# A new order for the opening of a hybrid encoder layer: contraction rows outside, rounding on ScalarE, sums on VectorE

## The chip, the cores and the metric

The kernel runs on one core of a Trainium2 chip. A time is the device time of one launch in microseconds (us); the measure is the median over several launches. One further launch is recorded by the hardware profiler, and all views of the profile are of that launch. "us from the start" counts from the first instruction of that record.

## The reference

One layer of a bidirectional encoder on x of 2048 rows and 1024 columns, in float32. Cut to what the change touches:

```python
mod = silu(c) @ w_mod + b_mod                       # 6 vectors of 1024: shift1, scale1, gate1, ...
hmix = rms_norm(x, g_norm1) * (1 + scale1) + shift1
proj = hmix @ w_in                                  # 2832 columns
q_a, k_a, v_a, q_m, k_m, v_m, o_m, gates = split(proj)
# windowed attention on q_a, k_a, v_a; two-way mLSTM on q_m, k_m, v_m with the 16 gate columns
x = x + gate1 * (concat(att, h_m) @ w_out)
x = x + gate2 * (silu(g) * u) @ w_ffn_out           # SwiGLU on a second modulated norm
return rms_norm(x) * g_final
```

So nothing of `proj` can be formed before `scale1` and `shift1` are there, and these need 8 MB of `w_mod` (two of its six blocks of 1024 columns, 4 MB each).

## The kernel before, in words

Every product is made to nearly float32 accuracy out of three products of a rounded type (`fp32r`): an operand t is split in a high part, t rounded, and a low part, t minus the high part, and `mm3` (L55 to L58) adds high x high, high x low and low x high. So each operand costs a rounding and a subtraction before TensorE can use it.

The first stage makes the columns of `proj` that are wanted with rows on the partitions: 272 (attention values, gates, one head of mLSTM values; tile `pa`) and 384 (the other mLSTM values; tile `pv`). `nat_mm` (L396) does this for one tile of 128 rows: for each of eight blocks k of the contraction three products into `pa`, then the same for `pv`. The weights of block k are the tiles `wnh` and `wnl` (high and low, split in `split_nat`, L339, from the raw `wnr`); the rows are the transposed, modulated x, the tiles `hT`.

A block of 512 rows of x (`xt`) is scaled by its inverse root mean square, and then for each k: four transposes on TensorE (L182), one ScalarE instruction that applies scale and shift and writes `ntmp` (L183), a VectorE copy that rounds (L189) and a VectorE subtraction (L190). All that is `turned_split` (L185).

The modulation is made in halves z of 512 columns, since block k = 4z..4z+3 needs half z only. `mod_sum` (L205) is a generator of three steps. The first multiplies the rows of `w_mod` by silu(c) and adds them up on VectorE (L212, L214: eight instructions for a whole sum). The second adds over the partitions on TensorE, directly to a column (L229), or, if the first four blocks are left to TensorE (`n_pe` is 4), by L219 and L220 to a row which ScalarE copies (L222) and L225 turns into a column. The third adds the bias (L236). With m = 1 for the scale and m = 0 for the shift, `n_pe` is 4 for (1, 0) and for (0, 1). `scales(z)` (L327) then makes the factor that L183 uses.

The order of the opening is written out (L403 to L437): both sums of half 0, the weights of half 0, blocks k = 0 to 3 of x, then all products of these four blocks for row tiles 0, 1 and 2, which have six banks of PSUM between them (`ops`); then half 1 of the sums, of the weights and of x. After L438 come the products of blocks 4 to 7 for tiles 0 to 2, then tiles 3 to 15. TensorE's order is the program's order throughout the kernel. The other engines keep the program's order up to L438 too; after it a planner places their instructions, and it can place them into gaps ahead of L438.

From L980 on the convolution tiles of the mLSTM are projected (L497, `proj_mm`), 24 products into a bank `g` of which there are two. ScalarE and VectorE empty it (L524, and L511, L512 in `sides`, seven products after its last). Beside this runs `gates` (L836): a chain of small VectorE and ScalarE steps with four little TensorE steps. It yields the number of the product at which its next step is put into every queue. `rps` (L885) adds chunk totals, a scan follows on eight partitions, `cps` (L899, L900) spreads the result, and at last the values are transposed (L924) and stored with four DMAs (L920, L921) for the mLSTM, whose first load of them (L602) comes after product 252. `w_out_ops` (L945) runs on GpSimd at the same time.

Of the kernel before, what the change touches and what calls it, by code (L numbers as in the profile page):

```python
# [11 lines left out]
F32 = mybir.dt.float32  # L12
# [9 lines left out]
P = 128  # L22
T = 2048
D = 1024
KT = D // P
# [11 lines left out]
def hybrid_layer_kernel(  # L37
# [14 lines left out]
    def bank(tag, name):  # L52
        return pp.tile([P, 512], F32, tag=tag, name=name, bufs={"g": 2, "a": 2, "b": 1, "c": 2, "d": 1}[tag])
# [108 lines left out]
    def squares(pl, xt):  # L162

        ssq = pl.tile([P, 4], F32, tag="ssq", name="ssq")
        for i in range(4):
            jk = pl.tile([P, D], BF16, tag="junk", name="junk", bufs=1)
            act.activation(jk, xt[i], AF.Square, accum_out=ssq[:, i:i + 1])
        return ssq

    def scaled(xt, r, on_act=False):  # L170

        for i in range(4):
            if on_act:
                act.activation(xt[i], xt[i], AF.Copy, scale=r[:, i:i + 1])
            else:
                dve.tensor_scalar(xt[i], xt[i], r[:, i:i + 1], None, MUL)
# [8 lines left out]
    def turned_split(pl, xt, k, gs, shift, dst):  # L185

        t = pl.tile([P, 512], F32, tag="ntmp", name="ntmp", bufs=2)
        turned(t, xt, k, "bd"[k % 2], gs, shift)
        dve.tensor_copy(dst(0, k), t)  # L189
        dve.tensor_tensor(dst(1, k), t, dst(0, k).bitcast(F32), SUB)  # L190
# [14 lines left out]
    def mod_sum(pl, m, z, ws_, n_pe):  # L205


        acc = pl.tile([P, 512], F32, tag="macc", name="macc")
        for k in range(n_pe, KT):
            w = ws_[k // 2][:, k % 2, :]  # L210
            if k == n_pe:
                dve.tensor_scalar(acc, w, sc_col[:, k:k + 1], None, MUL)  # L212
            else:
                dve.scalar_tensor_tensor(acc, w, sc_col[:, k:k + 1], acc, MUL, ADD)  # L214
        yield True
        if n_pe:
            ps = bank("b", "modrow")
            for k in range(n_pe):
                pe.matmul(ps[:1, :], sc_col[:, k:k + 1], ws_[k // 2][:, k % 2, :], start=k == 0, stop=False)  # L219
            pe.matmul(ps[:1, :], ones[:, 0:1], acc, start=False, stop=True)  # L220
            row = pl.tile([1, 512], F32, tag="mrow", name="mrow", bufs=1)
            act.activation(row, ps[:1, :], AF.Copy)  # L222
            ps = bank("b", "modps")
            for k in range(4):
                pe.matmul(ps[:, k:k + 1], row[:, k * P:(k + 1) * P], ones[:1, 0:1], start=True, stop=True)  # L225
        else:
            ps = bank("d", "modps")
            for k in range(4):
                pe.matmul(ps[:, k:k + 1], acc[:, k * P:(k + 1) * P], ones[:, 0:1], start=True, stop=True)  # L229
        yield True  # L230
        mod_bias(m, z, ps)
        yield True
# [44 lines left out]
    with tc.tile_pool(name="sw", bufs=2, side="right", reuse_waits="tile") as sw:  # L277
# [58 lines left out]
                sp.dma_start(r[1 + i], w4[:, 2 * i:2 * i + 2, C_VM:C_VM + 512])  # L336
            return r

        def split_nat(z, r):  # L339
            ks = BD[z]  # L340
            act.activation(wh[:, ks, :144], r[0], AF.Copy)
            dve.tensor_tensor(wl[:, ks, :144], r[0], wh[:, ks, :144].bitcast(F32), SUB)
            for i in range(4):
                k, v = 4 * z + i, r[1 + i // 2][:, i % 2]
                act.activation(wh[:, k, 144:], v, AF.Copy)
                (pool, dve)[i % 2].tensor_tensor(wl[:, k, 144:], v, wh[:, k, 144:].bitcast(F32), SUB)

        def norm1(n, xt):
            hT.append(Kt(n, f"hT{n}"))
# [58 lines left out]
        for src, o, n in ((g_norm2, O_G2, 8), (conv_b, O_CB, 8), (conv_w[0], O_CW, 24), (g_attn_out, O_GA, 4), (g_mlstm_out, O_GM, 4)):  # L408
            sp.dma_start(rows[1][o - N_A:o - N_A + n, :], src.rearrange("o (a b) -> (o a) b", b=P))
        hT.append(Kt(0, "hT0"))  # L410
        ms = {(m, z): mod_sum(s1, m, z, wm[m, z], 4 if m == 1 - z else 0) for z in range(2) for m in (1, 0)}
        ssq = squares(s1, xts[0])
        r = rsqrt(s1, ssq, 4, D, "rs")
        next(ms[1, 0])
        scaled(xts[0], r, True)
        next(ms[0, 0])
        next(ms[1, 0])
        next(ms[1, 0])
        next(ms[0, 0])
        next(ms[0, 0])  # L420
        scales(0)
        split_nat(0, wn[0])
        ops = {i: (bank("gga"[i], "pa"), bank("acc"[i], "pv")) for i in range(3)}
        for k in range(4):
            turned_split(s1, xts[0], k, gs1, mod[:, 0, :], hT[0])
        for i in range(3):
            deque(nat_mm(0, i, *ops[i], range(4)), 0)
        next(ms[1, 1])
        split_nat(1, wn[1])
        next(ms[1, 1])  # L430
        next(ms[1, 1])
        next(ms[0, 1])
        next(ms[0, 1])
        next(ms[0, 1])
        scales(1)
        for k in range(4, KT):
            turned_split(s1, xts[0], k, gs1, mod[:, 0, :], hT[0])  # L437
# [5 lines left out]
        for n in range(NB):  # L443
            if n + 1 < NB:
                nrm = norm1(n + 1, xts[n + 1])
                next(nrm)
            if n == 0:
                xts.append(load_x(3))
            if n == 1:
                vecs = mod_row(2)  # L450
                columns_of(1, N_A, N_B)
                dve.tensor_scalar(cvw, cols[:, O_CW:O_CW + 24].rearrange("p (j k) -> p j k", j=3), 0.5, None, MUL)
                dve.tensor_scalar(cvb, cols[:, O_CB:O_CB + KT], 0.5, None, MUL)
                dve.tensor_scalar(gml, cols[:, O_GM:O_GM + HM], 0.5, None, MUL)
            if n + 1 == NB:
                w_first = proj_cols(C_KM)
            for i in range(4):
                tt = 4 * n + i
                if tt < 3:
                    pa, pv = ops[i]  # L460
                else:
                    pa, pv = bank("g", "pa"), bank("a", "pv")
                ev = EVERY[n][i]
                for j, _ in enumerate(nat_mm(n, i, pa, pv, range(4 if tt < 3 else 0, KT))):
# [371 lines left out]
    def gates():  # L836
# [43 lines left out]
        for sl, j in ((lo_, 127), (hi_, 0)):  # L880
            dve.tensor_scalar(st[sl, 0], spot[sl], b[sl, j:j + 1], None, MUL)
            dve.scalar_tensor_tensor(st[sl, 1], spot[sl], cm[sl, j:j + 1], st[sl, 0], MUL, ADD)
        yield 62
        ps = bank("c", "rps")
        pe.matmul(ps[:8, :2 * NT], pick, st.rearrange("p j c -> p (j c)"), start=True, stop=True)  # L885
        sr = s2.tile([8, 2, NT], F32, name="sr", bufs=1)
# [3 lines left out]
        dve.tensor_copy(rw[:, 0, 1:], mn[:, :-1])  # L890
        dve.tensor_tensor(rw[:, 1], sr[:, 0], mn, SUB)
        dve.tensor_tensor(rw[:, 2], rw[:, 1], rw[:, 0], ADD)
# [4 lines left out]
        dve.tensor_tensor(rx, rowm, rw[:, 2].unsqueeze(1).to_broadcast([8, 8, NT]), MUL)  # L897
        ps = bank("c", "cps")
        pe.matmul(ps[:, :2 * NT], rowm.rearrange("q r c -> q (r c)"), rw[:, :2].rearrange("q j c -> q (j c)"), start=True, stop=True)  # L899
        pe.matmul(ps[:, P:2 * P], ones[:8, :], rx.rearrange("q r c -> q (r c)"), start=True, stop=True)  # L900
# [1108 lines left out]
```

## Time and profile before

| | |
|---|---|
| median of three runs (lowest, highest) | 2263.84 us (2262.03, 2265.5) |
| the profiled execution: time, span | 2262.92 us, 2261.1 us |
| TensorE busy | 2219.7 us, 98% |
| VectorE, ScalarE, GpSimd busy | 1611.6, 1061.4, 1041.5 us |

The difference between the profiled time and the span, 1.8 us, lies around the instructions. In a row of the timeline stand the start, the duration, the engine, the line, the operation, what it writes and reads, its shape, how many instructions the row takes together, and in brackets how long the engine had been idle and what ended that. In a row of the windows each engine has its busy time and number of instructions, then comes the granted clock of TensorE (1.00 is full), the share of the DMA engines and the rate. Matmuls overlap, so that the pace of a stream is the distance of the starts and not the duration.

### The profile page before, as it was taken

What the parts mean: (1) busy time and instruction counts of PE and PEld (TensorE: products, weight loads), DVE (VectorE), ACT (ScalarE), POOL (GpSimd) and SP (SyncE); (2) the same over time, 40 slices, a digit from 0 to 9 for tenths busy, and PEclk for the clock granted to TensorE, in tenths of its full rate; (3) what the DMA queues carried; (4) which work ended last, traced back from release to release, by engine and by line L of the source; (5) the groups of instructions that cost most, each with busy time, mean ns of one, the idle gap of its engine ahead of it and who ended that gap; (6) DMA issues with size and microseconds to landing.
All of it is one profiled execution on the core that took longest, in us unless ns stands there. A gap on an engine that the chain in (4) does not pass through costs nothing.

```text
span 2261.1 us, 32357 instructions
## 1 busy us (share of the span) xinstructions
PE 2219.7 (98%) x10818; PEld 1858.9 (82%) x10818; DVE 1611.6 (71%) x2942; ACT 1061.4 (47%) x2209; POOL 1041.5 (46%) x904
## 2 busy tenths in 40 slices
PE   7999999999999999999999999999999999999998
PEld 4997888888788878888888888888888888888887
DVE  6776667656688887886667777777766665785694
ACT  5433665554678746354445444433333333233452
POOL 1016535334344333436666565467665663692020
PEclk8999999999999999999999999999999999999999
DMA  8566755685766576764343455534333374543462
GB/s 323 169 208 200 227 166 170 190 241 168 209 185 189 175 242 209 266 234 156 107 144 110 153 182 170 170 126 140 98 112 98 112 260 141 172 149 95 145 217 93
DMA packets 337063, 391.28 MB, mean 173 GB/s; under 512 B 20874, under 2 KB 234234, under 8 KB 336896
## 3 DMA queue, kind: packets, MB, share of 16 engines
q1 hardware_dynamic: 335616, 388.65, 52.8%
q8 instruction: 85, 1.39, 0.3%
q14 instruction: 82, 0.67, 0.1%
q10 hardware_dynamic: 1280, 0.56, 0.1%
HBM read 269.95 MB, written 119.19 MB: 172 GB/s over the span
## 4 chain that ended last, share of the span: by engine, by line
PE 88%; DVE 5%; ACT 2%; DMA 2%; issue 1%; POOL 1%; SPq 0%; POOLq 0%; ACTq 0%; DVEq 0%
PE gps L497 15%; PE fp L56 12%; PE fp L57 12%; PE fp L58 12%; PE fo L58 5%; PE fo L57 5%; PE fo L56 5%; PE ops L56 2%; PE ops L58 2%; PE ops L57 2%; PE atp L807 1%; PE num L708 1%; PE kvp L621 1%; PE num L710 1%; PE pv L56 1%
## 5 line engine op out<-in xcount | busy, mean ns | idle before, releaser
L497 PE MATMUL gps<-hT,whi 128*128 128x512 f32 x1088 | 395.1, 418 | 0.0
L58 PE MATMUL fo<-w,al 128*128 128x512 f32 x616 | 239.8, 389 | 0.0
L56 PE MATMUL fo<-w,ah 128*128 128x512 f32 x616 | 239.7, 389 | 0.0
L57 PE MATMUL fo<-w,ah 128*128 128x512 f32 x616 | 239.7, 389 | 0.0
L497 PE MATMUL gps<-hT,wlo 128*128 128x512 f32 x544 | 226.1, 416 | 0.0
L497 PEld LDWEIGHTS gps<-hT,whi 128*128 128x128 f32 x1088 | 199.5, 189 | 23.5
L56 PE MATMUL fp<-T,S 128*128 128x512 f32 x528 | 206.7, 391 | 0.3 <-ACT s L1622 0.3
L57 PE MATMUL fp<-T,S 128*128 128x512 f32 x528 | 205.7, 389 | 0.0
L58 PE MATMUL fp<-T,S 128*128 128x512 f32 x528 | 205.4, 389 | 0.0
L1763 DVE TENSOR_TENSOR al<-al,ah 128x1024 fp32r<-128x1024 f32 x77 | 115.0, 1499 | 106.9 <-ACT ah L1762 106.7
L1762 ACT ACTIVATE ah<-al 128x1024 fp32r<-128x1024 f32 x77 | 81.7, 1060 | 181.5 <-DMA al<-a_d 175.9
L1465 DVE TENSOR_TENSOR S<-sf,S 128x512 fp32r<-128x512 f32 x86 | 126.9, 1513 | 37.1 <-ACT S L1464 36.9
L1465 DVE TENSOR_TENSOR A<-graw,A 128x512 fp32r<-128x512 f32 x86 | 128.9, 1518 | 16.7 <-ACT A L1464 16.6
L58 PE MATMUL fp<-B,A 128*128 128x512 f32 x352 | 136.9, 389 | 0.0
L56 PE MATMUL fp<-B,A 128*128 128x512 f32 x352 | 136.9, 389 | 0.0
L57 PE MATMUL fp<-B,A 128*128 128x512 f32 x352 | 136.9, 389 | 0.0
L58 PEld LDWEIGHTS fo<-w,al 128*128 128x128 f32 x616 | 115.6, 188 | 24.6 <-DVE al L1763 0.5
L56 PEld LDWEIGHTS fo<-w,ah 128*128 128x128 f32 x616 | 115.6, 188 | 24.1
L57 PEld LDWEIGHTS fo<-w,ah 128*128 128x128 f32 x616 | 115.6, 188 | 24.1
L800 POOL TENSOR_SCALAR ap<-ap,adn 128x384 f32<-128x384 f32 (+1 forms) x124 | 70.2, 585 | 132.2 <-PE atp L807 62.2
L1469 POOL TENSOR_TENSOR sf<-A,A22r 128x512 f32<-128x512 f32 x42 | 59.3, 1412 | 151.0 <-DMA A22r<-in_w_ffn_in_dram 134.5
L1632 DVE SCALAR_TENSOR_TENSOR g<-t,g 128x512 f32<-128x512 f32 x44 | 42.1, 957 | 114.0 <-ACT t L1631 114.0
(440 smaller groups left out, 6156.9 us busy)
## 6 DMA issues: line engine op xcount, KB each, us to landing
al<-a_d SPq DMA_DIRECT2D x77, 512.0 KB, 4.2
wmod<-in_w_mod_dram SPq DMA_DIRECT2D x48, 512.0 KB, 7.4
graw<-in_w_ffn_in_dram SPq DMA_DIRECT2D x43, 512.0 KB, 3.8
a_d<-ka SPq DMA_DIRECT2D x66, 256.0 KB, 4.9
bc<-bc_d SPq DMA_DIRECT2D x64, 256.0 KB, 4.8
hop_d<-n SPq DMA_DIRECT2D x56, 256.0 KB, 4.1
a_d<-u SPq DMA_DIRECT2D x55, 256.0 KB, 4.6
mqk<-qk_d SPq DMA_DIRECT2D x44, 256.0 KB, 4.5
```

What stands on the lines that cost most here:

```text
L56: pe.matmul(o, lh, rh, start=first, stop=False, skip_group_check=skip)
L57: pe.matmul(o, lh, rl, start=False, stop=False, skip_group_check=skip)
L58: pe.matmul(o, ll, rh, start=False, stop=last, skip_group_check=skip)
L497: pe.matmul(ps, w[i == 2][:, k, :], hT[n](i == 1, k), start=(k == 0 and i == 0), stop=(k == KT - 1 and i == 2))
L621: pe.matmul(kvp[:, :129], kn, vw, start=True, stop=True)
L708: pe.matmul(num[:, d, :129], sc[:, d, :], va_c, start=True, stop=st is None)
L800: pool.tensor_scalar(p, p, dn[:, g:g + 1], 0.0, MUL, ADD)
L1465: dve.tensor_tensor(t[:, 1, :], f, t[:, 0, :].bitcast(F32), SUB)
L1469: add.tensor_tensor(f1, a21, a22, ADD)
L1632: dve.scalar_tensor_tensor(g0, t0, 1.0, g0, ADD, MUL)
L1762: act.activation(ah, al.bitcast(F32), AF.Copy)
L1763: dve.tensor_tensor(al, al.bitcast(F32), ah.bitcast(F32), SUB)
```

## The change

In the opening of the first stage:

- The products of tiles 0, 1 and 2 are made with the contraction outside: all three tiles for block 0, then for block 1, and so on to block 5. Only blocks 6 and 7 of these tiles are left for the loop after L438 (`range(6 ...` in place of `range(4 ...`).
- The four transposes of a block (`trn`) are separate from the rest (`turn`, `low`) and are issued ahead, two blocks before the products that use them.
- The rounding of a block of x is a ScalarE copy in place of the VectorE copy; that of later rows (`turned_split` in `norm1`) stays on VectorE.
- The low parts of the weights are all made on VectorE (`small_lo`, `nat_lo`), where GpSimd made every other one.
- Both sums of half 1 are made on VectorE alone (`part_sum`, eight instructions each) and added over the partitions by four little products (`by_col`); TensorE's share of (0, 1) with its ScalarE copy is gone. `mod_sum` serves half 0 alone, with two other PSUM banks.
- These pieces are interleaved: one or two of the new sums stand between the first blocks, the rest behind block 3.

In `gates`, the step of `rps` moves from product 62 to 74, the exponential from 76 to 86, `rx` from 84 to 92; `cps`, which had shared the step of `rx`, has its own at 102, and the later steps move from 92, 100 and 112 to 110, 118 and 130.

```diff
-            ps = bank("b", "modps")
+            ps = bank("c", "modps")
...
-            ps = bank("d", "modps")
+            ps = bank("g", "modps")
...
-        ms = {(m, z): mod_sum(s1, m, z, wm[m, z], 4 if m == 1 - z else 0) for z in range(2) for m in (1, 0)}
+        ms = {m: mod_sum(s1, m, 0, wm[m, 0], 4 * m) for m in (1, 0)}
...
+        def turn(k):
+            t = s1.tile([P, 512], F32, tag="ntmp", name="ntmp", bufs=2)
+            act.activation(t, tps.pop(k), AF.Identity, bias=mod[:, 0, k:k + 1], scale=gs1[:, k:k + 1])
+            act.activation(h0(0, k), t, AF.Copy)
+            tps[k] = t
+
+        def low(k):
+            dve.tensor_tensor(h0(1, k), tps.pop(k), h0(0, k).bitcast(F32), SUB)
+
+        def prods(k, tiles):
+            for i in tiles:
+                deque(nat_mm(0, i, *ops[i], (k,)), 0)
...
+        trn(0)
+        trn(1)
+        nat_hi(0)
+        next(ms[0])
+        next(ms[1])
+        small_lo(0)
+        nat_lo(0)
+        next(ms[0])
         scales(0)
-        split_nat(0, wn[0])
+        nat_lo(1)
+        nat_lo(2)
         ops = {i: (bank("gga"[i], "pa"), bank("acc"[i], "pv")) for i in range(3)}
...
+        turn(0)
+        low(0)
+        nat_lo(3)
+        trn(2)
+        prods(0, range(3))
+        turn(1)
+        low(1)
+        part_sum(acc[0], 1, (0,))
+        trn(3)
+        prods(1, range(3))
+        turn(2)
+        low(2)
+        part_sum(acc[0], 1, (1,))
+        trn(4)
+        prods(2, range(3))
+        turn(3)
+        low(3)
+        part_sum(acc[0], 1, range(2, KT))
+        nat_hi(1)
+        ps = by_col(acc[0])
+        part_sum(acc[1], 0, range(4))
+        mod_bias(1, 1, ps)
+        prods(3, range(2))
+        part_sum(acc[1], 0, range(4, KT))
+        ps = by_col(acc[1])
+        prods(3, (2,))
+        small_lo(1)
+        nat_lo(4)
+        mod_bias(0, 1, ps)
         scales(1)
+        trn(5)
+        turn(4)
+        nat_lo(5)
+        low(4)
+        prods(4, (0,))
+        trn(6)
+        turn(5)
+        nat_lo(6)
+        low(5)
+        prods(4, (1, 2))
+        trn(7)
+        turn(6)
+        nat_lo(7)
+        low(6)
+        turn(7)
+        low(7)
+        prods(5, range(3))
...
-        yield 62
+        yield 74
...
-        yield 76
+        yield 86
...
-        yield 84
+        yield 92
...
+        yield 102
         ps = bank("c", "cps")
...
-        yield 92
+        yield 110
...
-        yield 100
+        yield 118
...
-        yield 112
+        yield 130
```

More of the change, by code (lines that the diff above doesn't have):

```diff
@@ L337, in load_nat, with nat_part, nat_hi, small_lo @@
             return r
-        def split_nat(z, r):
-            ks = BD[z]
[L341 to L346, printed above, removed]
+        def nat_part(k):
+            r = wn[k // 4]
+            return r[1 + k % 4 // 2][:, k % 2]
+        def nat_hi(z):
+            act.activation(wh[:, BD[z], :144], wn[z][0], AF.Copy)
+            for k in range(4 * z, 4 * z + 4):
+                act.activation(wh[:, k, 144:], nat_part(k), AF.Copy)
+        def small_lo(z):
+            ks = BD[z]
+            dve.tensor_tensor(wl[:, ks, :144], wn[z][0], wh[:, ks, :144].bitcast(F32), SUB)
+        def nat_lo(k):
+            dve.tensor_tensor(wl[:, k, 144:], nat_part(k), wh[:, k, 144:].bitcast(F32), SUB)
         def norm1(n, xt):
@@ L410, in hybrid_layer_kernel @@
         hT.append(Kt(0, "hT0"))
-        ms = {(m, z): mod_sum(s1, m, z, wm[m, z], 4 if m == 1 - z else 0) for z in range(2) for m in (1, 0)}
-        ssq = squares(s1, xts[0])
-        r = rsqrt(s1, ssq, 4, D, "rs")
[L414 to L420, printed above, removed]
+        ms = {m: mod_sum(s1, m, 0, wm[m, 0], 4 * m) for m in (1, 0)}
+        x0, h0 = xts[0], hT[0]
+        tps = {}
@@ new lines, in trn @@
+        def trn(k):
+            tps[k] = ps = bank("bd"[k % 2], "trn")
+            for i in range(4):
+                pe.transpose(ps[:, i * P:(i + 1) * P], x0[i][:, k * P:(k + 1) * P], ident)
+        def turn(k):
[5 more added lines that the diff above has]
+            dve.tensor_tensor(h0(1, k), tps.pop(k), h0(0, k).bitcast(F32), SUB)
@@ new lines, in prods, with part_sum, by_col @@
+        def prods(k, tiles):
+            for i in tiles:
+                deque(nat_mm(0, i, *ops[i], (k,)), 0)
+        def part_sum(acc, m, ks):
+            for k in ks:
+                w = wm[m, 1][k // 2][:, k % 2, :]
+                if k == 0:
+                    dve.tensor_scalar(acc, w, sc_col[:, k:k + 1], None, MUL)
+                else:
+                    dve.scalar_tensor_tensor(acc, w, sc_col[:, k:k + 1], acc, MUL, ADD)
+        def by_col(acc):
+            ps = bank("d", "modps")
+            for k in range(4):
+                pe.matmul(ps[:, k:k + 1], acc[:, k * P:(k + 1) * P], ones[:, 0:1], start=True, stop=True)
+            return ps
@@ L421, in hybrid_layer_kernel @@
+        ssq = squares(s1, x0)
+        r = rsqrt(s1, ssq, 4, D, "rs")
+        next(ms[1])
+        scaled(x0, r, True)
+        next(ms[0])
+        next(ms[1])
+        trn(0)
+        trn(1)
+        nat_hi(0)
+        next(ms[0])
+        next(ms[1])
+        small_lo(0)
+        nat_lo(0)
+        next(ms[0])
         scales(0)
-        split_nat(0, wn[0])
+        nat_lo(1)
+        nat_lo(2)
         ops = {i: (bank("gga"[i], "pa"), bank("acc"[i], "pv")) for i in range(3)}
-        for k in range(4):
-            turned_split(s1, xts[0], k, gs1, mod[:, 0, :], hT[0])
@@ L426, in hybrid_layer_kernel @@
[L426 to L434, printed above, removed]
-        scales(1)
-        for k in range(4, KT):
-            turned_split(s1, xts[0], k, gs1, mod[:, 0, :], hT[0])
+        acc = [s1.tile([P, 512], F32, tag="macc", name="macc") for _ in range(2)]
+        turn(0)
+        low(0)
+        nat_lo(3)
@@ L463, in hybrid_layer_kernel @@
                 ev = EVERY[n][i]
-                for j, _ in enumerate(nat_mm(n, i, pa, pv, range(4 if tt < 3 else 0, KT))):
+                for j, _ in enumerate(nat_mm(n, i, pa, pv, range(6 if tt < 3 else 0, KT))):
                     if ev and j % ev == ev - 1:
```

## The prediction

> **What bounds the kernel now.** I read the page first, then busy time by windows of 2 us over the first 62 us, then the timelines of the engines there, then the stretch around 190 us, where the windows show the next large hole.
>
> ```profile
> PE 2219.7 (98%) x10818; PEld 1858.9 (82%) x10818; DVE 1611.6 (71%) x2942; ACT 1061.4 (47%) x2209; POOL 1041.5 (46%) x904
> ```
>
> TensorE is busy for 98% of the span, 41 us of 2261.1 are idle. Work that TensorE doesn't have to do, or can do earlier, is therefore worth its full time at the end. The window rows show two more things:
>
> ```profile
> 24.00:26.00 2.00, 2.00 (x11) 2.00 (x11) 1.29 (x4) 1.82 (x4) 1.98 (x2) 0.50 1.05 407
> 28.00:30.00 2.00, 1.95 (x8) 1.27 (x6) 1.93 (x5) 0.69 (x1) 0.00 (x0) 0.50 1.14 354
> 34.00:36.00 2.00, 2.00 (x13) 2.00 (x13) 1.96 (x2) 0.33 (x1) 1.67 (x2) 0.94 1.05 407
> 50.00:52.00 2.00, 1.47 (x10) 1.23 (x11) 0.51 (x3) 1.20 (x2) 0.00 (x0) 0.83 0.00 0
> 54.00:56.00 2.00, 1.97 (x10) 1.42 (x8) 1.93 (x4) 1.97 (x4) 0.00 (x0) 0.82 0.79 270
> 180.00:200.00 20.00, 16.26 (x73) 12.74 (x72) 18.68 (x31) 6.50 (x14) 16.67 (x18) 1.00 0.61 192
> ```
>
> The last but two is the granted clock, the second the time TensorE was busy. It is half from 24 us, though TensorE counts as busy for all of 24 to 26. The means 0.94, 0.83 and 0.82 are mixtures of half and full, and put the changes at 34.24 (up), 51.32 (down) and 54.72 (up). With the drop at 24.0 the distances are 10.24, 17.08 and 3.40 us, that is 3, 5 and 1 times 3.41. So here the clock is decided on a grid: 24.0, 27.4, 30.8, 34.2, 37.7, 41.1, 44.5, 47.9, 51.3, 54.7. The last row, 180 to 200, has 3.74 us of idle TensorE.
>
> ```profile
> 24.53 3.93 PE L182 MATMUL trn<-ident,xt 128*128 128x128 f32 x16
> ...
> 33.15 0.52 PE L57 MATMUL pv<-wnl,hT 128*128 128x384 f32 x1
> 33.47 0.52 PE L58 MATMUL pv<-wnh,hT 128*128 128x384 f32 x1
> ...
> 43.67 3.59 PE L219 MATMUL modrow<-wmod,sc_col 128*1 128x512 f32 x8
> 48.80 1.05 PE L225 MATMUL modps<-ones_r,mrow 1*128 1x1 f32 x8 [0.68 <-ACT mrow L222]
> ...
> 53.85 0.43 PE L58 MATMUL pa<-wnh,hT 128*128 128x272 f32 x1
> 54.07 0.43 PE L56 MATMUL pa<-wnh,hT 128*128 128x272 f32 x1
> ...
> 65.45 0.34 PE L57 MATMUL pv<-wnl,hT 128*128 128x384 f32 x1
> 65.63 0.34 PE L58 MATMUL pv<-wnh,hT 128*128 128x384 f32 x1
> 65.80 0.29 PE L56 MATMUL pa<-wnh,hT 128*128 128x272 f32 x1
> 65.92 0.29 PE L57 MATMUL pa<-wnl,hT 128*128 128x272 f32 x1
> ```
>
> In this timeline of TensorE a product follows the last after 0.22 us (272 columns) or 0.32 us (384) at half clock, and after 0.12 and 0.175 at full clock. A transpose takes 0.245 us at half clock (3.93 over 16) and, by the same ratio, about 0.135 at full. The row at 65.80 is the first of tile 3: **tiles 0 to 2 end at 65.80, and the opening's gain is what this moves.**
>
> **The change, part by part: the opening.** Durations on VectorE and ScalarE:
>
> ```profile
> 17.83 5.47 DVE L214 SCALAR_TENSOR_TENSOR macc<-wmod,sc_col,macc 128x512 f32<-128x512 f32 x7
> ...
> 32.29 0.48 DVE L212 TENSOR_SCALAR macc<-wmod,sc_col 128x512 f32<-128x512 f32 x1
> 32.81 7.30 DVE L214 SCALAR_TENSOR_TENSOR macc<-wmod,sc_col,macc 128x512 f32<-128x512 f32 x7
> ...
> 40.69 1.29 DVE L346 TENSOR_TENSOR wnl<-wnr,wnh 128x512 fp32r<-128x512 f32 x2
> ...
> 49.96 0.15 DVE L327 SCALAR_TENSOR_TENSOR gs<-mod,cols 128x4 f32<-128x4 f32 x1
> 51.60 0.43 DVE L189 CAST hT<-ntmp 128x512 fp32r<-128x512 f32 x1 [1.49 <-ACT ntmp L183]
> 52.06 0.69 DVE L190 TENSOR_TENSOR hT<-ntmp,hT 128x512 fp32r<-128x512 f32 x1
> ```
>
> ```profile
> 23.18 2.45 ACT L345 ACTIVATE wnh<-wnr 128x512 fp32r<-128x512 f32 x4 [0.50 <-DMA wnr<-in_w_in_dram]
> 25.67 1.63 ACT L183 ACTIVATE ntmp<-trn,mod,gs 128x512 f32<-128x512 f32 x2
> ...
> 39.56 1.06 ACT L167 ACTIVATE junk<-xt 128x1024 bf16<-128x1024 f32 x1 [5.23 <-DMA xt<-in_x_dram]
> ```
>
> From these: a sum step 0.78 us (5.47 over 7), or 1.04 (7.30 over 7, with GpSimd at work beside the first half of it); a first step, which adds nothing, 0.5; a weight's low part 0.65 (1.29 over 2; the small one, with an eighth more columns, 0.75); the rounding copy on VectorE 0.43, the subtraction 0.69; on ScalarE `ntmp` 0.8 and a rounding copy 0.62 (2.45 over 4). I take ScalarE's copy of x at the weight's 0.62, the same shape and types.
>
> What leaves TensorE: from 43.67 to 49.85 it makes the column sums of (0, 1) and waits for them, 6.2 us. VectorE gets four more sum steps for it (3.1 us) and the four low parts that GpSimd had (2.6 us); it loses eight copies (3.4 us). ScalarE gets eight copies, 5.0 us, and loses one row copy. Through every queue, then, in the new order:
>
> 1. Half 0 is as before: its sum ends on VectorE at 23.3 (17.83 + 5.47), the columns are made on TensorE before the transposes at 24.53, so scale at 25.1. Transposes 0 and 1 now lie before that, where TensorE was idle. ScalarE's weights end at 25.63, `ntmp` and rounding of block 0 at 27.1, its low part at 27.8.
> 2. Transposes 2 at 26.5 to 27.5 at half clock, then 18 products of block 0. Their 9 + 9 cost 4.9 us at half and 2.7 us at full clock. In the row 28 to 30 the stream was not full, as each block of x was split only just ahead of its products; now one block feeds 18, so I let the grid window from 27.4 to 30.8 count as full and the clock rise at 30.8: products end at 31.7.
> 3. Transposes 3 stand behind these: 32.3. `ntmp`, rounding (1.45) and low part: 34.5. **This is the new wait.** VectorE has finished low parts 0 to 2 and two sum steps by 31.2, and its six next sum steps are queued behind low part 3.
> 4. Six steps end at 39.2, four of the shift's sum at 42.0, the bias, four more at 45.3. All data are there: the last of half 1's `w_mod` is queued ahead of the next x rows, whose first landed at 39.56 (ScalarE row). Two low parts and the bias follow: scale of half 1 at 47.05, against 50.11 (49.96 + 0.15).
> 5. TensorE meanwhile: blocks 1 and 2 till 38.2, the column at 39.2, two tiles of block 3 till 42.0, then nothing until 45.3. The window 41.1 to 44.5 has 0.9 us of work, so I take half clock from 44.5 till 51.3. Column till 46.65, rest of block 3 till 48.3, transposes 5 till 49.3.
> 6. Block 4's `ntmp`, rounding and low part: 47.1 to 49.2. Six products till 50.9, transposes 6 till 51.6, twelve products at full clock till 53.4, transposes 7 till 53.9, block 5 till 56.6. Low part 7 ends at 56.05 and is needed at 57. Blocks 6 and 7 of three tiles, 36 products, 5.4 us: 62.1.
>
> **So 62.1 in place of 65.8: 3.7 us earlier.** Ends for what the trace doesn't show: with the clock full from 30.8 on 61.1 (−4.7); with half clock one grid step longer, until 54.7, 63.7 (−2.1). With sum steps of 1.04 the thirteen on the path take 3.4 more and nearly all is gone (65.5); I take 0.78, since GpSimd has nothing to do here now. A delay between ScalarE's rounding and the `ntmp` that it reads isn't in the trace; the like pair on VectorE, 51.60 and 52.06, leaves 0.03, and it counts twice on the path: nothing to 0.1.
>
> The trace's drop at 51.3 follows a window (47.9 to 51.3) that was far from idle: it holds the row at 48.80 and most of the 1.47 us in the row 50 to 52. [...]
>
> Bank changes of the modulation columns cost nothing: both are free until the products take them, after 27 us.
>
> **The change, part by part: the gates.** TensorE and VectorE before:
>
> ```profile
> 189.24 0.61 PE L497 MATMUL gps<-hT,whi 128*128 128x512 f32 x2
> 191.52 0.23 PE L885 MATMUL rps<-st,pick 128*8 128x32 f32 x2 [1.66 <-DVE st L882]
> ...
> 196.93 0.40 PE L899 MATMUL cps<-rw,rowm 8*128 8x32 f32 x2
> 199.41 0.48 PE L900 MATMUL cps<-rx,ones_r 8*128 8x128 f32 x2 [2.08 <-DVE rx L897]
> ```
>
> ```profile
> 188.21 0.79 DVE L882 SCALAR_TENSOR_TENSOR st<-spot,gates,st 64x16 f32<-64x16 f32 x1
> ...
> 190.28 1.19 DVE L882 SCALAR_TENSOR_TENSOR st<-spot,gates,st 64x16 f32<-64x16 f32 x1
> ...
> 192.35 0.75 DVE L512 SCALAR_TENSOR_TENSOR cacc<-gps,cvw,cacc 128x511 f32<-128x511 f32 x1
> ...
> 196.04 1.15 DVE L892 TENSOR_TENSOR rw<-rw 8x16 f32<-8x16 f32 x1
> ...
> 198.62 0.73 DVE L897 TENSOR_TENSOR rx<-rowm,rw 8x128 f32<-8x128 f32 x1
> ```
>
> TensorE came to `rps` at 189.86 and got it at 191.52 (1.66 idle), and to `rx` at 197.3 and got it at 199.41 (2.08): the 3.74 of the window. A product is 0.227 us (0.68 for three). Twelve products later `rps` would be reached at 192.6, past 191.47, the end of `st`. But the block of products that begins at number 72 needs the bank that VectorE empties by the row at 192.35, which ends at 193.1. That was hidden in the wait; without it TensorE is there at 192.1 and waits 1.0. Then `rps` at 193.6, its chain ends at 197.2 as before (VectorE's queue holds it, not TensorE), the next emptying at 198.65, when TensorE reaches product 96 (198.75): no wait. `rx` now stands behind one more VectorE step and ends near 200.4; TensorE reaches `cps` at 200.1: 0.3. **Sum 1.3 in place of 3.74: 2.4 us less.** Ends: 3.7 if the bank is free in time, and 1.0 if GpSimd's work beside it stretches VectorE by another 1.4 us, as its 16-column step did here (1.19 at 190.28 against 0.79 at 188.21).
>
> The last step issues four DMAs and three transposes, 18 products or 4.1 us later.
>
> ```profile
> 246.57 0.43 SPq L602 DMA_DIRECT2D bc<-bc_d  x1
> ```
>
> TensorE comes to number 130 near 207, and the first reader of these stores is issued at 246.57: nothing. Loads and stores queued behind them on SyncE are now ahead of them.
>
> **Sum:** 3.7 + 2.4 = 6.1 us, from the profiled 2262.92 to 2256.8. The median of the runs is 0.92 higher, so 2257.7. I quote differences against the median.
>
> **The rivals.**
>
> (a) *The opening's gain is given back after it.* VectorE scales the next-but-one rows at 63.19, ahead of the first copy of the next block:
>
> ```profile
> 63.19 2.74 DVE L176 TENSOR_SCALAR xt<-xt,rsy 128x1024 f32<-128x1024 f32 x4
> ...
> 68.00 0.43 DVE L189 CAST hT<-ntmp 128x512 fp32r<-128x512 f32 x1 [2.07 <-ACT ntmp L183]
> ```
>
> This ended at 65.9 and TensorE needed nothing of it before 68. If tile 3 starts 3.7 us earlier and the planner leaves the order, its third `ntmp` buffer waits until 67.1, when TensorE wants transposes 4 at 67.3: some 0.6 to 1 us. If the squares of these rows are also placed between ScalarE's new copies, all 3.7 go. Then only the gates' 2.4 stay: 2261.4, within 0.2%. For it: ScalarE has 5 us more. Against: after the weights of half 1 (33.8 to 36.9) ScalarE is idle till 47, where squares fit, and the row at 39.56 shows one placed so.
>
> (b) *The clock stays at half* from 24 until blocks 6 and 7 are done, because TensorE's work now comes in pieces. Counted at half clock throughout: low part 3 at 35.6, scale at 50.4, block 5 ends at 64.5, and 36 products take 9.8: 74.3, or 8.5 later, less the gates' 2.4: 2269.9, slower. For it: in 28 to 30 TensorE counted 1.95 of 2.00 busy and the clock stayed at half until 34.24. Against: 51.3 to 54.7, transposes and products as now, was enough. It decides from the grid step at 58.1: if the clock rises only there, 36 products end at 65.4 and the opening gains nothing.
>
> (c) *Full clock and no gate wait:* 4.7 + 3.7 = 8.4 less, 2255.4.
>
> (d) *The gates' move does nothing* since VectorE's chain, not the numbers, sets the time; 3.7 less alone: 2260.1, inside 0.2%.
>
> **How the numbers follow.** 0.2% of the median is 4.5 us, about what a measurement of this kernel can tell from no change; the bounds are 2259.3 and 2268.4. Forecast (2254.5 to 2260) 0.48, of which 0.04 lie inside 0.2%; (c) 0.14; (a) 0.15; (d) 0.08; (b) and its like 0.15, of which 0.02 lie inside 0.2%. Faster 0.44 + 0.14 = 0.58, same 0.04 + 0.15 + 0.08 + 0.02 = 0.29, slower 0.13. The range runs from below (c), 2252.5, to 2265.5, past (a) and (d), and leaves (b) out with a little at the lower end; the forecast's own is 2254.5 to 2260.
>
> **What would show it.** The first product of tile 3 at 62 (right) or past 65 (wrong), and the gates' first transposes (L841) as much earlier. Scale of half 1 at 47. VectorE idle between 31 and 34 before low part 3. TensorE idle before `by_col` of the shift for 3 us. Half clock from 24.0 to 30.8 and 44.5 to 51.3. In the gates: no wait at `rps`, about 1 us ahead of the product after number 72, under 0.5 us at `cps`. Wrong would be the sum if the clock rows differ by a grid step or more, if ScalarE's planned squares stand between `turn` 4 and 7, or if a hole as large as the gain opens at tile 3 or behind it.

## The result, and the profile after

The changed kernel takes 2259.44 us (median of 22 runs, 2255.93 to 2263.72) against 2263.99 us of the kernel before (22 runs, 2261.81 to 2269.16) in the same session. The ratio is 0.998, with a 95% interval from 0.9974 to 0.9986: 4.55 us less, 3.2 to 5.9. The forecast was 6.1 us less. The interval holds it apart from no change. 0.2% of the time are 4.5 us, and so 2259.44 stands right at the border that the prediction drew between same and faster (2259.3), inside its own range (2254.5 to 2260) and near the slow end of it. The profiled execution of the changed kernel was the slowest of its 22 (2263.72, its span 2261.9), so positions inside it are compared with those of a second profile further down.

The opening came out in the order that the prediction walked through. VectorE in the timeline of the changed kernel (start, duration, engine, line, operation; in brackets the idle time ahead of it and what ended it):

```profile
34.43 0.69 DVE L434 TENSOR_TENSOR hT<-ntmp,hT 128x512 fp32r<-128x512 f32 x1 [3.30 <-ACT hT L430]
35.04 4.68 DVE L446 SCALAR_TENSOR_TENSOR macc<-wmod,sc_col,macc 128x512 f32<-128x512 f32 x6
...
42.51 3.11 DVE L446 SCALAR_TENSOR_TENSOR macc<-wmod,sc_col,macc 128x512 f32<-128x512 f32 x4
...
47.73 0.15 DVE L327 SCALAR_TENSOR_TENSOR gs<-mod,cols 128x4 f32<-128x4 f32 x1
```

The new wait ahead of low part 3 (3.30 us), sum steps of 0.78 us (4.68 over 6) and the scale of half 1 at 47.73 instead of 49.96 are there, 0.6 to 0.8 us later than forecast (low part 3 ends at 35.1, the scale at 47.9). ScalarE, in the same view, is not:

```profile
47.98 0.78 ACT L429 ACTIVATE ntmp<-trn,mod,gs 128x512 f32<-128x512 f32 x1 [6.56 <-DVE gs L327]
48.65 1.04 ACT L167 ACTIVATE junk<-xt 128x1024 bf16<-128x1024 f32 x1
49.60 0.19 ACT L167 ACTIVATION_READ_ACCUMULATOR junk<-xt 128x1 f32 x1
49.69 0.62 ACT L430 ACTIVATE hT<-ntmp 128x512 fp32r<-128x512 f32 x1
50.35 0.78 ACT L429 ACTIVATE ntmp<-trn,mod,gs 128x512 f32<-128x512 f32 x1
51.03 1.04 ACT L167 ACTIVATE junk<-xt 128x1024 bf16<-128x1024 f32 x1
51.98 0.19 ACT L167 ACTIVATION_READ_ACCUMULATOR junk<-xt 128x1 f32 x1
52.07 0.62 ACT L430 ACTIVATE hT<-ntmp 128x512 fp32r<-128x512 f32 x1
```

The planner put one square of later rows (L167, of row tiles 5 to 8) into each `turn`, between `ntmp` (L429) and its rounding copy (L430). A `turn` takes 2.33 us (47.98 to 50.31) instead of the 1.4 of its two copies. TensorE:

```profile
45.77 1.84 PE L451 MATMUL modps<-ones_r,macc 128*128 128x1 f32 x8 [2.97 <-DVE macc L446]
...
59.06 0.40 PE L58 MATMUL pa<-wnh,hT 128*128 128x272 f32 x1 [0.40 <-DVE hT L434]
...
63.96 0.29 PE L56 MATMUL pa<-wnh,hT 128*128 128x272 f32 x1
...
64.73 0.60 PE L182 MATMUL trn<-ident,xt 128*128 128x128 f32 x4
...
78.25 0.26 PE L309 MATMUL colps<-ident,rows 48*128 48x48 f32 x1 [3.14 <-ACT ntmp L183]
...
194.47 0.73 PE L579 MATMUL gps<-hT,whi 128*128 128x512 f32 x2 [1.19 <-DVE cacc L594]
195.13 0.23 PE L967 MATMUL rps<-st,pick 128*8 128x32 f32 x2
...
202.12 0.46 PE L983 MATMUL cps<-rx,ones_r 8*128 8x128 f32 x2
```

The first row is the forecast idle time ahead of the shift's columns. Tile 3 begins at 63.96, not at 62.1; it was 65.80 before. Then, 14 us later, the transposes of the columns (`colps`) wait 3.14 us, and they stand at 78.25. Before, they stood earlier:

```profile
77.90 0.26 PE L309 MATMUL colps<-ident,rows 48*128 48x48 f32 x1 [1.13 <-ACT ntmp L183]
```

So **in this execution the opening's 1.84 us were lost again by 78 us**. The last three rows of the fence above are the gates: 1.19 us of idle TensorE in place of 3.74, none of it at `rps` and `cps`. What holds `colps` is in the chain of work, cut to this stretch (start, duration, what), and in ScalarE's timeline, both of the changed kernel:

```profile
64.30 2.74 DVE xt L176 x4
...
72.53 0.28 DVE vs L560
72.84 4.33 DMA vst_d<-vs
77.31 0.11 issue
77.42 0.78 ACT ntmp L183
78.25 0.26 PE colps L309
```

```profile
74.76 0.49 ACT L563 ACTIVATE va<-pv 128x384 f32<-128x384 f32 x1
77.25 0.28 ACT L559 ACTIVATE vs<-pa 128x128 fp32r<-128x128 f32 x1 [2.00 <-DMA vst_d<-vs]
77.42 0.77 ACT L183 ACTIVATE ntmp<-trn,mod,gs 128x512 f32<-128x512 f32 x1
```

`vs` has one buffer. Its next copy (L559) has to wait until the store of the last one has landed, here 4.33 us after its issue (all 16 stores of this tile in this execution: 1.7 to 5.8, half of them within 2.6); and the last block's `ntmp`, which empties the bank for `colps`, is queued behind that copy. In the kernel before, the same copy waited 0.38 us (0.93 in a second profile of it).

### The profile page after: what moved, and what is told of

It reads as the page before. It is cut to its first block, busy times and chain, and to the rows that moved or that the text cites. A ratio compares the mean times of both kernels' runs of the same rounds, so it can differ in the third digit from the quotient of the medians.

```text
span 2261.9 us, 32339 instructions
## 1 busy us (share of the span) xinstructions
PE 2216.6 (98%) x10808; PEld 1861.0 (82%) x10808; DVE 1619.1 (72%) x2942; ACT 1065.5 (47%) x2216; POOL 1035.0 (46%) x900
## 4 chain that ended last, share of the span: by engine, by line
PE 87%; DMA 4%; DVE 4%; ACT 2%; issue 1%; SPq 0%; POOL 0%; ACTq 0%; POOLq 0%; DVEq 0%
PE gps L579 14%; PE fp L56 12%; PE fp L58 12%; PE fp L57 12%; PE fo L58 5%; PE fo L57 5%; PE fo L56 5%; PE ops L56 2%; PE ops L58 2%; PE ops L57 2%; PE atp L889 1%; PE num L790 1%; PE kvp L703 1%; PE num L792 1%; PE ao L902 1%
```

## The experiments

**The two halves of the change, each alone, and the changed kernel again.** The gates alone: the kernel before, with the new numbers.

```
-        yield 62
+        yield 74
...
-        yield 112
+        yield 130
```

> The kernel before with the later gate steps alone. By the prediction's sum: 2.4 us less than before (about 2261.6), no wait at rps, about 1 us of wait at the convolution product after number 72, under 0.5 us at cps. If VectorE's chain sets the time whatever the numbers are (rival d): within 0.7 us of before.

Measured: 2261.59 us against 2263.6, ratio 0.9989 (0.9979 to 0.9998): 2.0 us less. In the trace 1.06 us of idle TensorE are left of 3.74, all in one row; `rps` follows without a wait:

```profile
192.84 0.73 PE L497 MATMUL gps<-hT,whi 128*128 128x512 f32 x2 [1.06 <-DVE cacc L512]
193.50 0.23 PE L885 MATMUL rps<-st,pick 128*8 128x32 f32 x2
```

The opening alone is the changed kernel with the old numbers of the gates.

> The changed kernel with the old gate numbers, so the new opening alone. By the prediction's sum: 3.7 us less than before (about 2260.3), tile 3 from 62 us. By the rival that the opening's gain is given back behind it (a wait at colps, as the one profile of the changed kernel has it): within 1 us of before, although tile 3 begins 1.5 us or more earlier.

Measured: 2263.44 us, ratio 1.0002 (0.9993 to 1.0011). Tile 3's stretch is earlier, `colps` waits 2.24 us, and the time is that of the kernel before: the given-back case.

> The changed kernel once more, for a second profile. If the wait of 3.1 us at colps belongs to the kernel, it is there again within 0.7 us; if it was that one execution's (a late store), it is under 1.5 us, and the gates' first transposes begin 1.5 us or more before 175.4. Time: 4 to 5 us under before.

Measured: 2259.18 us, ratio 0.9979 (0.997 to 0.9987). `colps` waits 2.20 us here, between the two cases expected, and the gates begin at 173.84, 1.54 us ahead of the first profile of the kernel before (175.38), not behind it.

**The one buffer.** The changed kernel with one edit:

```
-  vs = sw.tile([P, KV, 2, HD], F32R, tag="vs", name="vs", bufs=1)
+  vs = sw.tile([P, KV, 2, HD], F32R, tag="vs", name="vs", bufs=2)
```

> The changed kernel with two buffers for the tile vs, so that ScalarE need not wait for the store of the last one ahead of block 7's ntmp. If that store is what holds the last transposes' bank: the wait at colps falls to 1.2 us or less, and the time is 1.5 to 3 us under the changed kernel's. If the wait is VectorE's backlog (squares and scaling of the next rows): it stays above 2 us and the time is the changed kernel's within 0.7 us.

Measured: 2255.75 us, ratio 0.9968 (0.9956 to 0.9981), 7.9 us below the kernel before. TensorE and ScalarE in its timeline:

```profile
76.14 0.26 PE L309 MATMUL colps<-ident,rows 48*128 48x48 f32 x1 [0.92 <-ACT ntmp L183]
```

```profile
72.07 0.31 ACT L559 ACTIVATE vs<-pa 128x128 fp32r<-128x128 f32 x1
...
75.31 0.78 ACT L183 ACTIVATE ntmp<-trn,mod,gs 128x512 f32<-128x512 f32 x1
79.65 0.28 ACT L559 ACTIVATE vs<-pa 128x128 fp32r<-128x128 f32 x1 [3.56 <-PE pa L58]
```

Block 7's `ntmp` no longer has the waiting copy of `vs` ahead of it; it starts at 75.31 instead of 77.42. Is this the change's own loss, or would the second buffer have helped any opening? The kernel before with that one edit:

> The kernel before, with a second buffer for `vs` and nothing else. Theory A, the store of `vs` became late work only because the changed opening brings ScalarE to tile 4's copy earlier: nothing to gain here, within 1 us of the kernel before (2263.6), and the wait ahead of the columns' transposes (`colps`) stays at 0.9 to 1.2 us. Theory B, the one buffer costs the same with any opening: 3.5 us less, 2260, with the wait at `colps` under 0.5.

Measured: 2262.46 us, ratio 0.9998 (0.9989 to 1.0007), the wait 0.92 us. No gain shows there (the interval runs from 2.5 us less to 1.6 more). And the opening alone (old gates) with it:

> The changed opening with the old numbers of the gates, and a second buffer for `vs`. Alone, with one buffer, the opening gave nothing (2263.44 against 2263.6). Theory A, it saves 2 to 3 us up to tile 3, and the store gives them back: 2260.5 (3 less), with the wait at `colps` near 0.9 us and the gates' first transposes at 173 to 173.5. Theory B, the opening itself is worth nothing and the second buffer helps elsewhere or only together with the gates' new numbers: over 2262.

Measured: 2260.83 us, ratio 0.9989 (0.998 to 0.9998), the wait 0.92 us. This is 3.4 us under the median of the kernel before of its session (2264.25), and 2.5 by the ratio, where one buffer gave nothing, though the gates begin at 173.88 and not by 173.5. So the wait for the store is a loss that the changed opening runs into, and the opening's gain is 2.5 to 3.4 us once it is gone (by the interval 0.5 to 4.5). The traces show this more sharply than the times: `colps` waits 2.20 to 3.14 us in all three profiles of the changed opening with one buffer and 0.92 in all three with two.

**The squares inside `turn`.** Two ways to take them out. Without them, in the changed kernel with the second buffer (it leaves out the squares for tiles 4 to 11 and takes a constant for their sums):

```
+            if n < 3:
+                ssq = s1.tile([P, 4], F32, tag="ssq", name="ssq")
+                pool.memset(ssq, float(D))
+            else:
+                ssq = squares(s1, xt)
...
```

> The changed kernel with a second buffer for `vs`, and without the squares of the rows of the second and third column of row tiles: a constant stands in place of their sums (so that part of the normalization is left out), and nothing takes ScalarE's time between a block's `ntmp` and its rounding copy in the second half. Theory A, those squares hold up the low parts 4 to 7 and so the products of tiles 0 to 2: a `turn` takes 1.4 us instead of 2.6, low part 7 ends at 56 to 57 instead of 59, tile 3 begins at 62 to 62.7 instead of 64, and the time is 1.5 us below the 2255.75 with two buffers: 2254.2. Theory B, TensorE would be late anyway, by its half clock or by VectorE: tile 3 stays past 63.5, and the time within 0.7 us of 2255.75.

Measured: tile 3's first transposes (L182, 0.77 us behind its first product) at 63.16 in place of 64.63, `colps` at 74.46 in place of 76.14. The squares hold up TensorE, by 1.5 to 1.7 us against this profile and by 0.9 to 1.1 against a second one of the same kernel (in the table further down). But the time is 2257.58 us (ratio 0.9972, 0.9962 to 0.9982), not 2254.2. The lead is there at the start of attention, 577.66 against 579.26, and then it is lost. TensorE, and windows of 2 us (PE busy; granted clock third from last), of the kernel without the squares:

```profile
577.66 0.45 PE L867 MATMUL as<-ak,aq 128*128 128x384 f32 x1 [1.03 <-DVE nmx L871]
582.96 0.41 PE L867 MATMUL as<-ak,aq 128*128 128x384 f32 x1 [2.05 <-DMA ak<-kst_d]
```

```profile
581.00:583.00 2.00, 0.04 (x1) 0.07 (x1) 0.34 (x2) 1.01 (x3) 1.38 (x3) 1.00 0.68 225
583.00:585.00 2.00, 1.03 (x5) 0.60 (x5) 1.31 (x4) 0.65 (x2) 0.90 (x2) 0.81 0.07 23
585.00:587.00 2.00, 2.00 (x5) 1.78 (x6) 1.07 (x3) 0.06 (x1) 0.00 (x0) 0.50 0.00 0
587.00:589.00 2.00, 2.00 (x7) 1.75 (x6) 0.59 (x3) 1.19 (x3) 0.00 (x0) 0.50 0.02 6
589.00:591.00 2.00, 2.00 (x9) 1.71 (x8) 1.39 (x6) 0.71 (x2) 0.00 (x0) 0.50 0.39 117
591.00:593.00 2.00, 2.00 (x14) 1.71 (x14) 1.08 (x4) 1.86 (x6) 0.00 (x0) 0.99 0.99 236
```

The load of the keys for attention's third block (`ak`; the expectations call them the first keys) holds TensorE for 2.05 us, and the idle stretch is followed by 6.8 us of half clock, at an estimated price of at most half of it, 3.4 us. In the kernel with the second buffer alone the wait was 0.73 us and the clock stayed at 1.00. Nothing of the code there differs.

The second way keeps all the work and writes the order on by hand to the end of tile 3:

> All the work, with a second buffer for `vs` and the order written out by hand to the end of tile 3: the squares for tiles 4 to 7 stand right behind the weights of half 1, in ScalarE's idle stretch from 37 to 47 us, those for tiles 8 to 11 behind tile 3, and the scaling for tiles 4 to 7 behind low part 7. Theory A: as without the squares, tile 3 at 62 to 62.7, and 2254.2, or 1.5 us less than with two buffers alone. Theory B, the planner had these engines' order right behind the opening, and a written one costs what it saves: a new wait of over 1 us at the first transposes for tiles 4 to 7 or at `colps`, and 2255.5 or more.

Measured: 2272.25 us, ratio 1.004 (1.0028 to 1.0053), **slower**. Tile 3's first transposes come at 62.98, as wished, but the hand-written order moves the squares for tiles 8 to 11 behind tile 3, and the scaling that follows them comes too late:

```profile
90.66 0.47 PE L182 MATMUL trn<-ident,xt 128*128 128x128 f32 x1 [11.56 <-DVE xt L176]
```

A new wait was expected, but not there and not of that size. So only the squares were moved, in the kernel with the second buffer:

```
+        early = {0: squares(s1, xts[1])}
...
         prods(5, range(3))
+        early[1] = squares(s1, xts[2])
         pre.close()
```

The first line stands behind the weights of half 1; `norm1` takes the sums made early in place of making them.

> The changed kernel with a second buffer for `vs`; all the squares are made, those for tiles 4 to 7 behind the weights of half 1 and those for tiles 8 to 11 behind the last `turn`, written there, and everything behind is left to the planner as before. Theory A: tile 3 begins at 62 to 62.7, the transposes of the columns (`colps`) at 74.5 to 75 as in the kernel without these squares (74.46), attention's first block at 577.7 to 578.2 (579.26 with the second buffer alone), and the median is 1 to 1.5 us lower than that of the kernel with the second buffer alone. Theory B: the scaling of the rows for tiles 4 to 7, ready earlier now, is put by the planner ahead of the last low parts on VectorE, and tile 3 begins past 63.5: within 0.7 us of it.

Measured: 2256.22 us, ratio 0.9969 (0.9958 to 0.9981). ScalarE with the first and the last square for tiles 4 to 7 and with a `turn`, and TensorE at tile 3 and `colps`:

```profile
40.19 1.06 ACT L167 ACTIVATE junk<-xt 128x1024 bf16<-128x1024 f32 x1 [4.10 <-DMA xt<-in_x_dram]
...
44.19 1.06 ACT L167 ACTIVATE junk<-xt 128x1024 bf16<-128x1024 f32 x1
...
47.01 0.78 ACT L429 ACTIVATE ntmp<-trn,mod,gs 128x512 f32<-128x512 f32 x1 [1.67 <-DVE gs L327]
47.82 0.63 ACT L430 ACTIVATE hT<-ntmp 128x512 fp32r<-128x512 f32 x1
```

```profile
62.42 0.60 PE L182 MATMUL trn<-ident,xt 128*128 128x128 f32 x4
...
74.20 0.26 PE L309 MATMUL colps<-ident,rows 48*128 48x48 f32 x1 [0.92 <-ACT ntmp L183]
```

Beside it, the kernel with the second buffer alone and the kernel before, again:

> The kernel with a second buffer for `vs` alone, beside the one with the squares moved: 2255.75 again within 1.5 us. If the start of attention, not the opening, sets a part of the time, then this profile's wait for the first keys of `kst_d` (0.73 the first time) is anywhere from 0.7 to 2.2 us and the granted clock behind it 1.0 or under 0.9, whatever came before; attention's first block at 579 to 581.

Measured: 2257.18 us, ratio 0.9974 (0.9964 to 0.9984); the wait for the same keys is 1.78 us this time with the clock at 1.00 behind it, and what the expectations call attention's first block stands at 578.33, somewhat ahead of the expected 579.

> The kernel before, for a second profile of it. If the grid of the clock lies differently against the program in each execution, the drops and rises of the opening stand 3.41 us apart as before (24.0, 34.2, 51.3, 54.7) but all shifted by a common amount of up to 3.4 us, and tile 3 and the first block of attention (584.72) move by 1 to 3 us with it. If the grid is tied to the program, the drops stand at the same times within 0.3 us.

Measured: 2264.6 us, ratio 1.0002 (0.9994 to 1.0011). The granted clock drops at 23.45, 33.69 and 81.47 us and rises at 30.27, 37.10 and 84.89: all are whole multiples of 3.41 us apart, but they are not those of the first profile (24.0, 34.24, 51.31, 54.72) shifted by one amount: the phase is another, and with it the windows that fall to half. Tile 3's first transposes are at 68.52 instead of 66.55.

With the squares moved, tile 3 and `colps` are where theory A has them, or 0.3 us ahead; attention's first block is 0.3 us behind, at 578.47. The squares moved are 1.0 us below the second buffer alone, with intervals that overlap: a gain in the trace, not one that the times show. Both lie 7.3 to 8.2 us under the kernel before in the same session, where the changed kernel lay 4.4 and 4.55 under it in its sessions.

## Why the prediction was right and where it was wrong

One profile of each kernel was not enough to read single microseconds from, so here are all of them side by side. Positions are starts of TensorE's rows in us: the first transposes for tiles 4 to 7 (L182), `colps` with its wait, the gates' first transposes, and a row at the start of attention (`as`): the eighth scores, the first that wait for VectorE. Attention's first scores stand 5.6 to 6.4 us ahead of that row, which the expectations call attention's first block.

| kernel | L182 | `colps` (wait) | gates | `as` |
|---|---|---|---|---|
| before | 66.55 | 77.90 (1.13) | 175.38 | 584.72 |
| before, again | 68.52 | 80.42 (1.68) | 178.76 | 587.48 |
| gates alone | 66.96 | 78.21 (1.03) | 175.03 | 581.54 |
| before, two `vs` | 65.93 | 77.08 (0.92) | 173.90 | 583.45 |
| changed | 64.73 | 78.25 (3.14) | 176.54 | 583.69 |
| changed, again | 64.47 | 77.03 (2.20) | 173.84 | 580.82 |
| opening alone | 63.80 | 76.41 (2.24) | 174.68 | 584.51 |
| changed, two `vs` | 64.63 | 76.14 (0.92) | 172.95 | 579.26 |
| the same again | 64.03 | 75.54 (0.92) | 172.35 | 578.33 |
| opening alone, two `vs` | 65.52 | 77.06 (0.92) | 173.88 | 584.61 |
| no squares, two `vs` | 63.16 | 74.46 (1.00) | 171.28 | 577.66 |
| written on | 62.98 | 75.64 (0.92) | 187.37 | 593.98 |
| squares moved, two `vs` | 62.42 | 74.20 (0.92) | 171.01 | 578.47 |

**The gates (2.4 us): right.** Idle time there went from 3.74 to 1.19 (1.3 was forecast), at the forecast place: nothing at `rps`, 1.19 at the block behind product 72, which waits for VectorE to empty its bank; at `cps`, where 0.3 was forecast, nothing. From the gates' first transposes to the row `as` is 409.6 us in the mean of the five profiles of the table with the old numbers (408.7 to 410.7) and 406.7 in that of the eight with the new ones (406.0 to 407.5): 2.9 less. So rival (d), that the numbers change nothing, did not come. The prediction's lower bound for this gain (1.0 us) took VectorE's step of 1.19 us for one stretched by GpSimd and that of 0.79 for one that was not; GpSimd was at work beside both (187.29 to 191.44 without a pause), so that stretch is not shown.

**The opening (3.7 us): the step that failed.** The forecast had tile 3 at 62.1, so its transposes at 62.85. The six profiles of the changed opening with squares in `turn` have them at 64.53 in the mean (63.80 to 65.52), against 66.99 for the four of the old one (65.93 to 68.52): 2.5 us earlier. In the three kernels without squares in `turn`, they stand at 62.85 in the mean (62.42 to 63.16). So step 6 was worked out right for a `turn` of 1.4 us; what failed was that it counted `ntmp` and rounding of blocks 4 to 7 as neighbours on ScalarE. The squares between them cost 1.7 us. The prediction named the case, as what would make the sum wrong and inside rival (a), and set it aside because ScalarE is idle from 37 to 47 us. There is room for the squares there: written there by hand, all four for tiles 4 to 7 ran from 40.19 to 45.35, with one wait of 0.40 us for their rows behind the first. But room was not enough: in the changed kernel the first one starts at 40.27, the planner put only this one there, and the next ones beside the copies. Why it did so is not shown.

**The give-back: foreseen as rival (a), but it came through another wait.** Rival (a) let the scaling of the next rows on VectorE delay the first splits for tiles 4 to 7, 0.6 to 1 us, at transposes 4. The scaling is in the chain (64.30, 2.74 us), but TensorE waits for nothing there. The loss is at `colps` and behind it: from L182 to the gates the changed opening with one buffer needs 110.7 us (mean of three), with two buffers 108.3 (mean of three), and the old opening 109.0 with one buffer (mean of three) and 108.0 with two (one profile). The store's landing time was nowhere in the prediction's sum. The row that could have shown it, 0.38 us for `vst_d` on ScalarE before, was small because ScalarE came to that copy at 76.14, and at 75.25 in the changed kernel, while the store was issued only 0.5 us earlier (72.84 against 73.33) and landed later (77.2 against 76.5). Rival (a)'s scaling has a part in that: the chain above runs from it, over steps of VectorE and ScalarE, to the second half of `vs` (L560, 72.53) that the store has to wait for.

Part of the 2.4 us between one buffer and two is half clock behind the wait. In two of the three profiles with one buffer, that of the changed kernel (from 79.88 to 83.29) and that of the opening alone, the clock is at half for 3.4 us there, and from `colps` to the gates they need 98.3 us; the third, and all with two buffers but the one written on, need 96.8. The second profile of the kernel before has such a stretch too (81.47 to 84.89, and 98.3 us). Whether a longer wait makes it likelier is not shown.

**Clock: the period was right, the grid was not fixed.** The prediction took the drops and rises of one profile as times of the program. They lie on a 3.41 us period in every profile, but not at one phase: the first drop of the thirteen profiles is anywhere from 21.4 to 24.9 us, and the two profiles of the changed kernel have it at 21.85 and 24.90. All nine profiles of the changed opening have 17.1 us of half clock ahead of tile 3, not the 13.6 forecast, and the old opening 10.2 to 13.7. The three kernels without squares in `turn` reach tile 3 at the forecast place with 17.1 us of half clock too; whether the 3.4 us more fell into TensorE's waits, or something else ran faster than forecast, the runs do not separate. Windows of the grid of the kernel with the squares moved (PE busy first, clock third from last) show a drop:

```profile
37.03:40.44 3.41, 2.29 (x18) 2.01 (x18) 3.27 (x6) 0.25 (x1) 0.00 (x0) 1.00 1.04 420
40.44:43.85 3.41, 2.44 (x9) 1.93 (x8) 3.30 (x6) 2.94 (x5) 0.00 (x0) 0.50 1.03 417
43.85:47.27 3.42, 2.46 (x11) 2.49 (x12) 2.63 (x7) 1.67 (x5) 0.00 (x0) 0.50 0.98 402
47.27:50.68 3.41, 3.41 (x15) 3.15 (x14) 2.79 (x13) 2.41 (x4) 0.00 (x0) 0.50 0.11 41
```

A window that was busy for 2.29 of 3.41 us was followed by half clock, so were two more with 2.44 and 2.46, and after one that was busy throughout the clock was full. The prediction took the clock of a step from how busy the window before it was (full from 30.8, half from 44.5); that was its author's estimate. In this execution it does not hold throughout: a later window of the same grid was busy for less than the first row, 1.96 us, and the clock stayed full.

```profile
579.75:583.16 3.41, 1.96 (x11) 1.22 (x10) 0.85 (x5) 3.06 (x10) 0.73 (x2) 1.00 0.80 250
583.16:586.57 3.41, 2.08 (x9) 1.60 (x10) 1.97 (x5) 0.71 (x2) 1.54 (x3) 1.00 0.15 47
```

So in these profiles the busy share of a window alone does not say whether the clock drops; what does stays open. Rival (c), full clock from 30.8 us on, came in no profile of the changed opening; rival (b), half clock till tile 3 is done, did not come either, as the clock was full from 50.7 to 53.8 us on in every profile of the changed opening.

**The sum.** From the table: 2.5 gained up to L182, 1.6 given back up to the gates (110.7 against 109.0), 2.9 gained behind, 3.8 in all; 4.55 and 4.4 were measured. The two halves alone gave 2.0 and 0.2 us, with intervals about 4 us wide that leave room for the whole. The prediction's 6.1 contained 1.2 us too much for the opening as far as tile 3, lacked the 1.6 of the give-back, and had 0.5 too little for the gates. That the time still lies in the forecast's own range is luck in part: of the 3.7 us of the opening 0.9 were left at the gates, and the gates' larger gain and the width of the range made up for it.

**What stays open.** Why the load of the keys at the start of attention takes longer in some executions, and what drops the clock behind it in some. From the row `as` to the end the thirteen profiles need 1674.6 to 1678.9 us, with the same code there. The wait for this load alone doesn't explain it: the profile with the shortest (0.73 us) needs 1677.2, one with 1.80 needs 1675.7. Undoing the rounding on ScalarE alone, or the sums on VectorE alone, was not tried.

## What to carry to other kernels

Where a planner fills gaps, price a new chain of short steps with the planner's work in its gaps, not as neighbours; and when an order is written by hand over it, move one kind of work at a time (moving only the squares kept the time; writing the whole order on put a hole of 11.56 us elsewhere). A one-buffer tile that is stored by DMA is a hidden wait for the store's landing (4.33 us after its issue in the profile with the longest such wait, 2.00 us) in the queue of the engine that refills it: when a change brings work forward, look at which small waits in the rows of before can grow (0.38 us became 1.1 to 2.0). For a change of two or three microseconds, compare positions in several profiles of each kernel, up to where the next wait lies that differs between executions of one kernel (here the load of the keys, 0.73 and 1.78 us in the two profiles of the kernel with the second buffer).

## What was not expected of the hardware

- The phase of the clock's 3.41 us grid differs between executions of one kernel (first drop at 21.85 and 24.90 us in the two profiles of the changed kernel), and a window two thirds busy (2.29 of 3.41 us), in the second profile of the kernel before one of 82% (2.79 of 3.42, from 30.27 to 33.69), was followed by half clock, while one busy for 1.96 of 3.41 us was followed by full clock.
- A wait of TensorE for the same load at the start of attention was 0.73 to 2.18 us in these profiles, and was followed by up to 6.8 us of half clock in one execution and by none in another.
